# Modulation chunk 23 of layer 0 moves from TensorE to VectorE, and the first two down chunks are taken in turn by quarters

## The chip, the core and the metric

The kernel runs on one core of a Trainium2 chip. The metric is the device time of one execution in microseconds (us). The engines are named as in the profile: PE is TensorE, PEld its weight loads, DVE is VectorE, ACT is ScalarE, POOL is GpSimd, SP is SyncE, whose queue (SPq) issues the weight loads by DMA.

## The reference

A diffusion backbone of two layers over 256 latent tokens (`x`) and 256 context tokens (`ctx`), width D = 2048, inner width F = 5504. Layer 0 has a pooling mixer, layer 1 neighbourhood attention; each is followed by a gated feed-forward net with a width-3 convolution on its gate. Each layer has six modulation vectors of 2048 values per stream, from the condition vectors:

```python
ml = (silu_c @ w_mod[i] + b_mod[i]).reshape(B, 6, 1, D)
mc = (silu_cc @ w_mod[i] + b_mod[i]).reshape(6, 1, 1, D)
...
h = h + ml[:, 5] * conv_ffn(modulate(rms_norm(h, norm2_g[i]), ml[:, 3], ml[:, 4]),
                            ffn_w_gate[i], ffn_w_up[i], ffn_conv_w[i], ffn_conv_b[i], ffn_w_down[i])
if not last:
    ...
    hc = hc + mc[5] * conv_ffn(modulate(rms_norm(hc, norm2_g[i]), mc[3], mc[4]), ...)
```

The context rows go through the same weights, so both streams stand side by side as 512 columns.

## The kernel before

**Tiles.** Everything is kept transposed, features on the 128 partitions and the 512 token columns on the free axis. D is 16 input tiles (k), F is 43 tiles (f). A product of one f tile, gate (g) or up (u), takes 16 inputs; a "down" product goes the other way. Every product is three fp32r passes: high part by high, high by low, low by high, so a tile's gate has 48 matmuls. `split()` makes the two parts of a weight in SBUF: ACT casts it to the high part (L172), VectorE subtracts to get the low part (L174). It takes the buffers in turn from three pairs in `whp` and, once `extra` holds it, a fourth pair in `whx`. An input A or an activation `act` is split the same way (A: ACT L419 and DVE L420, from `nrm`, L417; `act`: ACT L513 and DVE L514).

**Weight loads.** `stage()` (L131) gives the staging buffer that has been free longest, and `load()` (DMA at L154) fills it with 512 KB. Up to the end of layer 0's partial stage, and on until `in_turn` is cleared, the loads are issued on SP's one queue in the order of the code; six `wst` buffers feed the last group.

**Modulation.** The 12,288 values of a layer are 24 chunks of 512; chunks 20 to 23 are the output gate `ml[:, 5]`, and chunk 20 + q scales the quarter q of a down chunk's output tiles (L919). In layer 0 a chunk is summed on TensorE by `mod_pe` (L228) in four steps: 1 MB is loaded (two DMAs), and eight matmuls of 32 output rows (`mod<-wm,sc`, L241) follow each step (up to chunk 20 two steps are taken together); then ACT copies the sums out (`modev`, L256), four transposes (`modt<-ident,modev`, L263) and a VectorE reduction (`modT`, L265) bring them to one column per k tile. In layer 1 the chunks are summed on VectorE by `mod_pairs` (L268): a weight tile times the condition value is added to `macc` (L299 and L301), and two STREAM_TRANSPOSE and TENSOR_REDUCE (L311, L312) and a matmul with `quad` (`quarter_sum`, L197) end it.

**Partial stage.** Gate and up of the tiles 0 to 7 are computed in four groups g while the mixer makes their inputs four at a time (`partial`, L686; matmuls L732 to 734). Tiles 0 to 5 keep their partial sums in SBUF (`part`, L747), tiles 6 and 7 in PSUM banks. At its side run `pw` (weights times shift, L714), its transposes `ptu`/`ptg` (L752) and sums `puu` (L759). A weight load of this stage is called `wcg_0`, `wcg_4`, `wcu_0` or `wcu_4` (gate or up, first or second four tiles). `between(half)` stands ahead of every half product: it pulls the modulation steps forward to a fixed rate (`need`, L785), 20 steps over the 32 halves of a group, and in the last group makes the second norm's scale (`n2v`, L390 to L392), normalises the inputs 0 to 11, and runs the gates of tiles 0 to 3 (`GATES`, halves 16, 19, 22 and 25). A gate (`gate0`, L497) needs the tile's `late` values (the norm's scale, L484 or L490, and the shift on ACT), two `g` operations on VectorE (L501, L503), a silu on ACT (L506), a product `sg` (L507) and the two parts of `act`.

**After the partial stage.** The main sequence (L923 on) makes the last four inputs and tile 6's gate, computes gate and up of tile 8 (`gu0`, L829, matmuls L844 to L846), then down chunk 0 (the tiles 0 to 3): four quarters `mg` of 48 matmuls (`down0`, L857; L907 to L909), whose weights of two loads each are split like the others. Each of the four outputs of a quarter is scaled on ACT (`dy`, L919) and added to `hl` and `hc` on GpSimd (L920). The gates of tiles 4 to 8 run between these quarters. Tiles 9, 10 and 11 follow, then down chunk 1 (the tiles 4 to 7), then the tiles 12 on. Layer 1's chunks (`pump`) start on VectorE with tile 12.

Of the kernel before, what the change touches and what calls it, by code (L numbers as in the profile page):

```python
# [17 lines left out]
P = 128  # L18
# [20 lines left out]
GATES = (16, 19, 22, 25)  # L39
# [20 lines left out]
def kernel(ctx: ExitStack, tc: tile.TileContext, xT, cxT, wmod, wg, wu, wd, wp,  # L60
# [97 lines left out]
    casts = []  # L158

    def split(ts, name, share=0, keep=False):  # L160

        parts = []
        for j, (t, n) in enumerate(ts):
            turn[0] += 1
            pools = [whp] * 3 + extra
            pool = pools[turn[0] % len(pools)]
            hi = pool.tile([P, 1024], F32R, tag="wh", name=f"{name}h{j}")
            lo = pool.tile([P, 1024], F32R, tag="wl", name=f"{name}l{j}")
            with ExitStack() as behind:
                for ins in hold:  # L170
                    behind.enter_context(tc.issue_after(ins))
                casts.append(nc.scalar.copy(hi[:, :n], t[:, :n]).ins)  # L172
                eng = nc.gpsimd if share and turn[0] % share == 0 else nc.vector
                eng.tensor_tensor(lo[:, :n], t[:, :n], hi[:, :n].bitcast(F32), op=ALU.subtract)  # L174
            parts.append((hi, lo))
        if not keep:
            used(ts)
        return parts
# [18 lines left out]
    def quarter_sum(x, n, name):  # L197


        ps = bank("d", f"{name}s")  # L200
        nc.tensor.matmul(ps[:, : 16 * n].rearrange("p (k s) -> p k s", s=n), quad, x, start=True, stop=True)
        v = ps[:, : 16 * n].rearrange("p (i b s) -> p i b s", b=4, s=n)
        return [v[32 * b : 32 * b + 32, :, b, :] for b in range(4)]
# [64 lines left out]
    def mod_pairs(todo, ring):  # L268
# [5 lines left out]
        def fetch(l, ch, m, streams, piece):  # L274
            tag = ring[len(loaded) % len(ring)]
            w = wst.tile([P, 1024], F32, tag=f"wst{tag}", name=f"wm{l}_{ch}_{piece}")
            if m == 1:
                g, j = divmod(2 * piece, 4)
                nc.sync.dma_start(w, wmod[l, ch, g, :, 512 * j : 512 * j + 1024])
# [9 lines left out]
        for i, (l, ch, m, streams, piece) in enumerate(steps):  # L289
            n = len(streams)  # L290
            while len(loaded) < min(i + 1 + ahead, len(steps)):
                fetch(*steps[len(loaded)])
            if piece == 0:
                acc = mp.tile([P, 1024], F32, tag="macc", bufs=1, name=f"macc_{l}_{ch}")
                acc = [acc, acc] if m == 2 else [acc[:, 0:512], acc[:, 512:1024]]
            for k, v in loaded[i]:
                for s in streams:
                    if k == 0:
                        nc.vector.tensor_scalar(acc[s], v, sc2[:, k, s : s + 1], None, op0=ALU.mult)  # L299
                    else:  # L300
                        nc.vector.scalar_tensor_tensor(acc[s], v, sc2[:, k, s : s + 1], acc[s],  # L301
                                                       op0=ALU.mult, op1=ALU.add)
            if ending is not None:
                ending()
                ending = None
            if piece == 8 * m - 1:
                r = mp.tile([P, 2, 16, 2], F32, tag="modr", bufs=2, name=f"modr_{l}_{ch}")
                for c in range(m):
                    for s in streams:
                        t = f0.tile([P, 512], F32, tag="t2", name=f"modu{s}_{l}_{ch}_{c}")  # L310
                        nc.vector.transpose(t, acc[s][:, 512 * c : 512 * c + 512])  # L311
                        nc.vector.tensor_reduce(out=r[:, c, :, s], in_=t.rearrange("p (k r) -> p k r", r=32),  # L312
                                                axis=AX.X, op=ALU.add)

                def ending(l=l, ch=ch, m=m, streams=streams, n=n, r=r):
                    for c in range(m):
                        finish_mod(l, ch + c, streams, quarter_sum(r[:, c, :, 0:n], n, f"modt_{l}_{ch + c}"))
            yield
        ending()
# [86 lines left out]
    A = {}  # L406

    def normalise(l, which, h_of, streams, rstd, pool, ks=range(KT), keep=A):

        for k in ks:  # L410
# [11 lines left out]
            keep[k] = a  # L422
            if l == 1 and k == 1:
                hold[:] = [ins.ins]
# [25 lines left out]
    with ExitStack() as ph0:  # L450
# [46 lines left out]
        def gate0(f, pg, pu):  # L497
# [10 lines left out]
            if f == NS - 1:  # L508
                a = mp.tile([P, 2, 512], F32R, tag="macc", bufs=1, name=f"act_{f}")
# [11 lines left out]
        with ExitStack() as phs:  # L521
# [37 lines left out]
            def mods():  # L559
# [6 lines left out]
                for q in range(4):  # L566
                    yield from mod_pe(0, 20 + q, sc, f0)
# [208 lines left out]
            for g in range(4):  # L776
# [8 lines left out]
                def between(half):  # L785
                    need(min(20 * g + LEAD + RATE * (half + 1) // 32, 20 * g + LEAD + PMAX))
# [25 lines left out]
            need(97)  # L812
# [7 lines left out]
        extra.append(whx)  # L820
# [4 lines left out]
        pump = mod_pairs([x for t in zip(two, one) for x in t], ring)  # L825

        tail = []

        def gu0(f):  # L829
            res = []  # L830
            for nm, wsrc in (("g", wg), ("u", wu)):
                parts = ld(wsrc[0, f], f"w{nm}0_{f}")
                if f > NS + 3:
                    next(pump, None)
                ps = bank("gu", f"{nm}0_{f}")
                for k in range(KT):
# [3 lines left out]
                    with ExitStack() as behind:  # L840
                        if f == NS and k == 0:
# [6 lines left out]
                    if k == 7 and f > NS + 3:  # L848
                        next(pump, None)
                res.append(ps)  # L850
# [6 lines left out]
        def down0(c, fs, acts, after=None):  # L857
            n = len(fs)
            last = c == len(chunks) - 1
            for mg in range(4):  # L860
# [34 lines left out]
                for m in range(4):  # L895
# [3 lines left out]
                    for i in range(n):  # L899
# [3 lines left out]
                        with ExitStack() as behind:  # L903
                            if c == 0 and i == 0:
# [4 lines left out]
                        nc.tensor.matmul(ps, lo[:, o : o + P], xh, start=False, stop=(i == n - 1))  # L909
# [11 lines left out]
                if after is not None:  # L921
                    after()
# [5 lines left out]
        res = gu0(NS)  # L928
        rest = [e for e in range(NS) if e not in acts]

        def more():
            e = rest.pop(0) if rest else None
            if e is not None:
                acts[e], _ = gate0(e, *late(e))

        while rest and rest[0] < 4:
            more()

        down0(0, chunks[0], [acts[f] for f in chunks[0]], more)
        while rest:  # L940
            more()
        acts[NS], sg = gate0(NS, *res)
        for c, fs in enumerate(chunks):
            if c < 2:
                continue
            if c == 3:
                in_turn.clear()
                rooms[:] = [r for r in rooms if -r not in ring]
# [677 lines left out]
```

## Time and profile before

| | |
|---|---|
| median of 3 runs | 3034.51 us (3032.35 to 3036.01) |
| profiled execution | 3033.66 us, span 3031.6 us, mean granted clock 0.996 |
| PE | 2971.9 us busy, 98% of the span |
| DVE, ACT, POOL | 64%, 45%, 26% of the span |
| DMA | 561.8 MB, 184 GB/s over the span |

The partial stage's last group runs from about 330 to 413 us of the span, tile 8 from 413 to about 439, down chunk 0 behind it. The page gives busy shares of each engine, the chain of work that ended last, and groups of instructions by line; rows of the timeline give start, duration, engine, line, output and inputs by the program's names (numbers left out where a row stands for several), and in brackets the idle time before the instruction and what ended it. A matmul's duration in a row overlaps its neighbours', so costs on PE are taken from start to start.

### The profile page before, as it was taken

The page shows a single profiled execution, that of the slowest core. Times are in us where ns is not written, and L with a number is a line of the kernel's source. Part 1 is how long each engine was busy: PE and PEld are TensorE (multiplying, and loading weights), DVE is VectorE, ACT ScalarE, POOL GpSimd, SP SyncE. Part 2 cuts the span into 40 slices and gives each one's busy share as a digit, 9 for nine tenths or more (in the row PEclk, how much of TensorE's full clock was granted, in tenths as well). Part 3 has the DMA queues.
Part 4 walks back from the last instruction along what each step waited for, and adds up shares of the span by engine and source line. Part 5 has one row for each costly group of instructions (what it writes and reads, how often), then busy time and mean ns, then how long its engine had stood idle before and what let it go on. Part 6 is the DMA issues. An engine that isn't in the chain of part 4 may idle for free.

```text
span 3031.6 us, 40905 instructions
## 1 busy us (share of the span) xinstructions
PE 2971.9 (98%) x15136; PEld 2413.7 (80%) x15136; DVE 1944.3 (64%) x2818; ACT 1377.2 (45%) x2234; POOL 797.7 (26%) x782
## 2 busy tenths in 40 slices
PE   5999999999999999999999999999999999999998
PEld 2666668888888888888888888878888888888887
DVE  4455674376584857658485657474778666666666
ACT  4433454324333242433334534343546566566665
POOL 0000003303123030311305002020003565566665
PEclk9999999999999999999999999999999999999999
DMA  9798653374665847566482433333346565555563
GB/s 395 283 363 317 231 193 98 115 245 150 204 203 165 236 148 235 159 202 209 152 257 78 127 99 123 107 120 112 112 151 204 172 199 190 193 182 188 183 193 118
DMA packets 178935, 561.81 MB, mean 185 GB/s; under 512 B 17712, under 2 KB 22576, under 8 KB 178736
## 3 DMA queue, kind: packets, MB, share of 16 engines
q1 hardware_dynamic: 178736, 559.19, 56.7%
q8 instruction: 120, 1.97, 0.3%
q14 instruction: 79, 0.65, 0.1%
HBM read 557.03 MB, written 2.10 MB: 184 GB/s over the span
## 4 chain that ended last, share of the span: by engine, by line
PE 94%; DMA 2%; POOL 1%; ACT 1%; DVE 1%; SPq 0%; issue 0%; DVEq 0%; ACTq 0%; POOLq 0%
PE g L1123 5%; PE u L1123 5%; PE d L907 5%; PE d L908 5%; PE d L909 5%; PE d L1176 4%; PE u L844 4%; PE u L845 4%; PE u L846 4%; PE g L845 4%; PE g L846 4%; PE g L844 4%; PE g L1126 3%; PE u L1126 3%; PE mod L241 2%; PE d L1180 2%
## 5 line engine op out<-in xcount | busy, mean ns | idle before, releaser
L920 POOL TENSOR_TENSOR hl<-hl,dy 128x256 f32<-128x256 f32 x160 | 148.4, 928 | 1010.4 <-ACT dy L919 1010.2
L1192 POOL TENSOR_TENSOR hl<-hl,dy 128x256 f32<-128x256 f32 x320 | 323.0, 1045 | 214.7 <-ACT dy L1190 212.4
L301 DVE SCALAR_TENSOR_TENSOR macc<-wm,sc,macc 128x512 f32<-128x512 f32 (+1 forms) x360 | 326.5, 937 | 72.2 <-DMA wm<-wmod 71.3
L919 ACT ACTIVATE dy<-d,modT 128x256 f32<-128x256 f32 x320 | 133.4, 470 | 187.5 <-PE d L909 169.2
L920 POOL TENSOR_TENSOR hc<-hc,dy 128x256 f32<-128x256 f32 x160 | 128.6, 803 | 0.0
L174 DVE TENSOR_TENSOR wd_2l<-wd,wd_2h 128x1024 fp32r<-128x1024 f32 (+1 forms) x44 | 55.6, 1270 | 108.2 <-ACT wd_2h L172 107.0
L1190 ACT ACTIVATE dy<-d,modT 128x512 f32<-128x512 f32 x160 | 104.6, 685 | 43.3 <-PE d L1180 41.8
L174 DVE TENSOR_TENSOR wd_3l<-wd,wd_3h 128x1024 fp32r<-128x1024 f32 (+1 forms) x44 | 53.4, 1234 | 77.3 <-ACT wd_3h L172 75.9
L241 PE MATMUL mod<-wm,sc 128*32 128x512 f32 x768 | 97.3, 624 | 5.6 <-DMA wm<-wmod 4.3
L1278 POOL TENSOR_TENSOR rk<-rk,rp 128x256 f32<-128x256 f32 x16 | 14.8, 927 | 317.4 <-DVE rk L1277 205.3
L174 DVE TENSOR_TENSOR wd_1l<-wd,wd_1h 128x1024 fp32r<-128x1024 f32 (+1 forms) x44 | 53.7, 1224 | 57.1 <-ACT wd_1h L172 57.1
L392 POOL TENSOR_TENSOR n2v<-n2v,minus_half 128x4 f32<-128x4 f32 x1 | 1.0, 1012 | 317.5 <-DMA wm<-wmod 317.5
L172 ACT CAST wd_1h<-wd 128x1024 fp32r<-128x1024 f32 (+1 forms) x44 | 45.3, 1031 | 77.5 <-PE u L845 53.1
L174 DVE TENSOR_TENSOR wd_0l<-wd,wd_0h 128x1024 fp32r<-128x1024 f32 (+1 forms) x44 | 53.2, 1220 | 27.5 <-ACT wd_0h L172 27.5
L1368 ACT ACTIVATE sb<-sb,nm 128x512 f32<-128x512 f32 x64 | 46.3, 723 | 51.7 <-DVE nm L1364 51.1
L907 PE MATMUL d<-act,wd_2h 128*128 128x512 f32 x172 | 67.1, 390 | 0.0
L908 PE MATMUL d<-act,wd_2h 128*128 128x512 f32 x172 | 66.9, 389 | 0.0
L909 PE MATMUL d<-act,wd_2l 128*128 128x512 f32 x172 | 66.9, 389 | 0.0
L907 PE MATMUL d<-act,wd_0h 128*128 128x512 f32 x172 | 66.9, 389 | 0.0
L908 PE MATMUL d<-act,wd_0h 128*128 128x512 f32 x172 | 66.9, 389 | 0.0
L909 PE MATMUL d<-act,wd_0l 128*128 128x512 f32 x172 | 66.9, 389 | 0.0
L907 PE MATMUL d<-act,wd_1h 128*128 128x512 f32 x172 | 66.9, 389 | 0.0
(1794 smaller groups left out, 9219.7 us busy)
## 6 DMA issues: line engine op xcount, KB each, us to landing
wm<-wmod SPq DMA_DIRECT2D x384, 512.0 KB, 6.4
wd<-wd SPq DMA_DIRECT2D x168, 512.0 KB, 4.4
wg<-wg SPq DMA_DIRECT2D x156, 512.0 KB, 4.6
wu<-wu SPq DMA_DIRECT2D x156, 512.0 KB, 4.6
wv<-wv SPq DMA_DIRECT2D x32, 512.0 KB, 4.0
wk<-wq SPq DMA_DIRECT2D x32, 512.0 KB, 4.0
wq<-wq SPq DMA_DIRECT2D x32, 512.0 KB, 3.8
wo<-wo SPq DMA_DIRECT2D x31, 512.0 KB, 4.5
```

Source lines behind the costliest of these rows:

```text
L174: eng.tensor_tensor(lo[:, :n], t[:, :n], hi[:, :n].bitcast(F32), op=ALU.subtract)
L301: nc.vector.scalar_tensor_tensor(acc[s], v, sc2[:, k, s : s + 1], acc[s], op0=ALU.mult, op1=ALU.add)
L844: nc.tensor.matmul(ps, hi[:, c : c + P], xh, start=(k == 0), stop=False)
L845: nc.tensor.matmul(ps, hi[:, c : c + P], xl, start=False, stop=False)
L846: ins = nc.tensor.matmul(ps, lo[:, c : c + P], xh, start=False, stop=(k == KT - 1))
L907: nc.tensor.matmul(ps, hi[:, o : o + P], xh, start=(i == 0), stop=False)
L908: nc.tensor.matmul(ps, hi[:, o : o + P], xl, start=False, stop=False)
L909: nc.tensor.matmul(ps, lo[:, o : o + P], xh, start=False, stop=(i == n - 1))
L920: nc.gpsimd.tensor_tensor(h_of(s)[:, k, :], h_of(s)[:, k, :], y[:, s], op=ALU.add)
L1123: nc.tensor.matmul(ps, hi[:, c : c + P], flat(B[k]), start=(k == 0), stop=False)
L1126: nc.tensor.matmul(ps[:, T:], lo[:, c : c + P], B[k][:, 0], start=False, stop=(k == KT - 1))
L1192: nc.gpsimd.tensor_tensor(hl[:, k, :], hl[:, k, :], y[:, q], op=ALU.add)
```

## The change

Chunk 23 is no longer summed by `mod_pe` (`LATER`). `mod_pairs` sums it for both streams on VectorE: eight loads of 512 KB into a ring of three `wst` buffers, 32 operations on `macc` (in `whx`'s buffer "wh"), two transposes and two reductions. Its pieces are advanced with tile 9 and with the down quarters, and each is ordered behind the last low part that was issued before it. Its quarter sum on TensorE stands behind quarter 2 of down chunk 1. The rate of the pumped steps in the last group goes from 20 to 15 over 32 halves.

The gates of tiles 0 to 3 leave `between`; they and tile 7's run behind tile 8's products, and 4, 5 and 8 behind tile 9's. Gate and up of tile 9 come ahead of the down chunks, and down chunks 0 and 1 are taken in turn: quarter 0 of chunk 0, quarter 0 of chunk 1, quarter 1 of chunk 0, and so on. `act_6` and `act_7` live in `whx`'s "wl" and in `mp`'s "macc", so `whx` joins `split()`'s turn only behind tile 11: until then there are three pairs. From tile 9 on the ring's three buffers are no rooms for weight loads. `in_turn` is cleared behind the quarters.

```diff
-GATES = (16, 19, 22, 25)
+LATER = (23,)
...
                 for q in range(4):
-                    yield from mod_pe(0, 20 + q, sc, f0)
+                    if 20 + q not in LATER:
+                        yield from mod_pe(0, 20 + q, sc, f0)
...
-                    need(min(20 * g + LEAD + RATE * (half + 1) // 32, 20 * g + LEAD + PMAX))
+                    need(20 * g + LEAD + (RATE if g < 3 else 19 - 4 * len(LATER)) * (half + 1) // 32)
...
-                    if g == 3 and half in GATES:
-                        e = GATES.index(half)
-                        acts[e], _ = gate0(e, *late(e))
...
-            need(97)
+            need(97 - 4 * len(LATER))
...
-        extra.append(whx)
...
+        endings = []
+        first_pump = mod_pairs([(0, ch, 1, both) for ch in LATER], ring, (whx, "wh"), last_low, endings)
...
             for k, v in loaded[i]:
                 for s in streams:
...
+                    with ExitStack() as behind:
+                        for x in (start, low_of) if home else ():
+                            behind.enter_context(tc.issue_after(x[-1]))
...
-        res = gu0(NS)
-        rest = [e for e in range(NS) if e not in acts]
...
-        while rest and rest[0] < 4:
-            more()
-
-        down0(0, chunks[0], [acts[f] for f in chunks[0]], more)
-        while rest:
-            more()
-        acts[NS], sg = gate0(NS, *res)
+        res = [gu0(NS)]
+        for e in (NS - 1, 0, 1, 2, 3):
+            acts[e], _ = gate0(e, *late(e))
+        rooms[:] = [r for r in rooms if -r not in ring]
+        res.append(gu0(NS + 1))
+        for e in (4, 5):
+            acts[e], _ = gate0(e, *late(e))
+        acts[NS], _ = gate0(NS, *res[0])
+        for mg in range(4):
+            for c in range(2):
+                down0(c, chunks[c], [acts[f] for f in chunks[c]], (mg,))
+                next(first_pump, None)
+                if (mg, c) == (2, 1):
+                    endings.pop(0)(tail)
+        acts[NS + 1], _ = gate0(NS + 1, *res[1])
+        in_turn.clear()
         for c, fs in enumerate(chunks):
             if c < 2:
                 continue
...
-            fs = [f for f in fs if f > NS]
+            fs = [f for f in fs if f > NS + 1]
             for f in fs:
                 acts[f], sg = gate0(f, *gu0(f))
+            if c == 2:
+                extra.append(whx)
+                continue
             down0(c - 1, chunks[c - 1], [acts[f] for f in chunks[c - 1]])
```

**SP's queue at the start of the last group, before** (chunk 20's loads `wm_20_...` and the first up weights `wcu_0`):

```order
L154 DMA wm_20_0_0_2899<-wmod 128x1024
L154 DMA wm_20_0_1024_2901<-wmod 128x1024
L154 DMA wm_20_1_0_2935<-wmod 128x1024
L154 DMA wm_20_1_1024_2937<-wmod 128x1024
L154 DMA wm_20_2_0_2965<-wmod 128x1024
L154 DMA wm_20_2_1024_2967<-wmod 128x1024
L154 DMA wcu_0_0_2992<-wu 128x2x512
L154 DMA wcu_0_1024_2994<-wu 128x2x512
```

The same place with the change:

```order
L154 DMA wm_20_0_0_2899<-wmod 128x1024
L154 DMA wm_20_0_1024_2901<-wmod 128x1024
L154 DMA wcu_0_0_2976<-wu 128x2x512
L154 DMA wcu_0_1024_2978<-wu 128x2x512
L154 DMA wm_20_1_0_2988<-wmod 128x1024
L154 DMA wm_20_1_1024_2990<-wmod 128x1024
L154 DMA wm_20_2_0_3033<-wmod 128x1024
L154 DMA wm_20_2_1024_3035<-wmod 128x1024
```

The two loads of `wcu_0` have moved ahead of four loads of chunk 20.

**SP's queue ahead of the stage's last weights `wcu_4`, before:**

```order
L154 DMA wm_22_2_0_3292<-wmod 128x1024
L154 DMA wm_22_2_1024_3294<-wmod 128x1024
L154 DMA wm_22_3_0_3320<-wmod 128x1024
L154 DMA wm_22_3_1024_3322<-wmod 128x1024
L154 DMA wm_23_0_0_3361<-wmod 128x1024
L154 DMA wm_23_0_1024_3363<-wmod 128x1024
L154 DMA wcu_4_0_3391<-wu 128x2x512
L154 DMA wcu_4_1024_3393<-wu 128x2x512
```

With the change:

```order
L154 DMA wm_21_2_0_3202<-wmod 128x1024
L154 DMA wm_21_2_1024_3204<-wmod 128x1024
L154 DMA wm_21_3_0_3231<-wmod 128x1024
L154 DMA wm_21_3_1024_3233<-wmod 128x1024
L154 DMA wm_22_0_0_3270<-wmod 128x1024
L154 DMA wm_22_0_1024_3272<-wmod 128x1024
L154 DMA wcu_4_0_3300<-wu 128x2x512
L154 DMA wcu_4_1024_3302<-wu 128x2x512
```

`wcu_4` stands a whole chunk earlier in the sequence of the chunk loads: behind the first step of chunk 22 and not of chunk 23.

**VectorE's order where tile 8's last inputs (`A_0_3_...`) are made, before** (`wd_0_0l` is a low part of down chunk 0's first weights, `g_6`, `sg` and `late` belong to tile 6's and 7's gates):

```order
L174 TENSOR_TENSOR wd_0_0l_3724<-wd_0_0_0_3719,wd_0_0h_3723 128x1024
L420 SCALAR_TENSOR_TENSOR A_0_3_3555<-nrm_3556,modT_15_2894,A_0_3_3555 128x256 x2
L420 SCALAR_TENSOR_TENSOR A_0_3_3563<-nrm_3564,modT_15_2894,A_0_3_3563 128x256
L503 SCALAR_TENSOR_TENSOR g_6_3571<-late_0_3403,vt_71,g_6_3571 128x2x255
L420 SCALAR_TENSOR_TENSOR A_0_3_3563<-nrm_3564,modT_15_2894,A_0_3_3563 128x256
L417 SCALAR_TENSOR_TENSOR nrm_3582<-hl,modT_19_2759,n2acc 128x256
L417 SCALAR_TENSOR_TENSOR nrm_3582<-hc,modT_19_2759,n2acc 128x256
L417 SCALAR_TENSOR_TENSOR nrm_3590<-hl,modT_19_2759,n2acc 128x256
L417 SCALAR_TENSOR_TENSOR nrm_3590<-hc,modT_19_2759,n2acc 128x256
L507 TENSOR_TENSOR sg_3575<-sg_3575,late_1_3551 128x512
L420 SCALAR_TENSOR_TENSOR A_0_3_3581<-nrm_3582,modT_15_2894,A_0_3_3581 128x256 x2
L420 SCALAR_TENSOR_TENSOR A_0_3_3589<-nrm_3590,modT_15_2894,A_0_3_3589 128x256 x2
```

With the change (its line numbers: `nrm` L434, low part of A L437, `late` L508, gate L521 and L525, low part of a weight L175):

```order
L521 SCALAR_TENSOR_TENSOR g_6_3464<-late_0_3312,vt_71,g_6_3464 128x2x255
L434 SCALAR_TENSOR_TENSOR nrm_3475<-hl,modT_19_2759,n2acc 128x256
L434 SCALAR_TENSOR_TENSOR nrm_3475<-hc,modT_19_2759,n2acc 128x256
L434 SCALAR_TENSOR_TENSOR nrm_3483<-hl,modT_19_2759,n2acc 128x256
L434 SCALAR_TENSOR_TENSOR nrm_3483<-hc,modT_19_2759,n2acc 128x256
L437 SCALAR_TENSOR_TENSOR A_0_3_3456<-nrm_3457,modT_15_2894,A_0_3_3456 128x256 x2
L175 TENSOR_TENSOR wu_8l_3560<-wu_8_1024_3553,wu_8h_3559 128x1024
L525 TENSOR_TENSOR sg_3468<-sg_3468,late_1_3444 128x512
L508 TENSOR_TENSOR late_0_3612<-cg_998,n2acc 128x512
L508 TENSOR_TENSOR late_1_3616<-cu_1270,n2acc 128x512
L437 SCALAR_TENSOR_TENSOR A_0_3_3474<-nrm_3475,modT_15_2894,A_0_3_3474 128x256 x2
L437 SCALAR_TENSOR_TENSOR A_0_3_3482<-nrm_3483,modT_15_2894,A_0_3_3482 128x256 x2
```

The two `late` operations of tile 7 now stand between tile 6's gate and the last inputs, and the 1024 low part there is tile 8's own.

On PE the down quarters of the change run with the first half's parts for three output tiles (18 matmuls of tiles 0 and 1 of the chunk's four) ahead of the second half's.

More of the change, by code (lines that the diff above doesn't have):

```diff
@@ L195, in by_row, with quarter_sum @@
         return ps.rearrange("p (i j c) -> p i c j", i=4, j=4)[:, :, 0:2, :]
-    def quarter_sum(x, n, name):
+    def quarter_sum(x, n, name, last=()):
         ps = bank("d", f"{name}s")
-        nc.tensor.matmul(ps[:, : 16 * n].rearrange("p (k s) -> p k s", s=n), quad, x, start=True, stop=True)
+        with ExitStack() as behind:
+            for ins in last:
+                behind.enter_context(tc.issue_after(ins))
+            nc.tensor.matmul(ps[:, : 16 * n].rearrange("p (k s) -> p k s", s=n), quad, x, start=True, stop=True)
         v = ps[:, : 16 * n].rearrange("p (i b s) -> p i b s", b=4, s=n)
@@ L278, in fetch @@
                 g, j = divmod(2 * piece, 4)
-                nc.sync.dma_start(w, wmod[l, ch, g, :, 512 * j : 512 * j + 1024])
+                with ExitStack() as behind:
+                    for ins in fetched[-1:] if home or (l, ch) == (1, 0) else ():
+                        behind.enter_context(tc.issue_after(ins))
+                    nc.sync.dma_start(w, wmod[l, ch, g, :, 512 * j : 512 * j + 1024])
                 loaded.append([(2 * piece + i, w[:, 512 * i : 512 * i + 512]) for i in range(2)])
@@ L507, in gate0 @@
             nc.vector.tensor_tensor(sg, sg, pu, op=ALU.mult)
-            if f == NS - 1:
-                a = mp.tile([P, 2, 512], F32R, tag="macc", bufs=1, name=f"act_{f}")
+            if f in (NS - 2, NS - 1):
+                pool, tag = (whx, "wl") if f < NS - 1 else (mp, "macc")
+                a = pool.tile([P, 2, 512], F32R, tag=tag, bufs=1, name=f"act_{f}")
             else:
@@ L840, in gu0 @@
                     with ExitStack() as behind:
-                        if f == NS and k == 0:
+                        if f <= NS + 1 and k == 0:
                             for x in tail:
@@ L849, in gu0 @@
                         next(pump, None)
+                    elif k == 7 and f == NS + 1:
+                        next(first_pump, None)
                 res.append(ps)
```

51 lines of the change are left out of this document (27 added, 24 removed).

## The prediction, as put on record

> **What bounds the kernel now.** I read the page first, for the busy shares and the chain that ended last.
>
> ```profile
> PE 2971.9 (98%) x15136; PEld 2413.7 (80%) x15136; DVE 1944.3 (64%) x2818; ACT 1377.2 (45%) x2234; POOL 797.7 (26%) x782
> PE 94%; DMA 2%; POOL 1%; ACT 1%; DVE 1%; SPq 0%; issue 0%; DVEq 0%; ACTq 0%; POOLq 0%
> ```
>
> TensorE (PE) is the bound nearly everywhere, so an edit is worth the TensorE work it removes plus the TensorE waits it ends. The table by stage, around the end of the partial stage, shows where waits are left (columns: stretch, its length, busy us of PE, PEld, DVE, ACT, POOL, granted clock, DMA share, GB/s).
>
> ```profile
> 340.00:350.00 10.00, 7.67 (x35) 4.45 (x34) 5.70 (x14) 1.91 (x3) 1.01 (x1) 0.83 0.17 67
> 390.00:400.00 10.00, 7.18 (x50) 3.48 (x50) 9.99 (x21) 9.94 (x20) 0.00 (x0) 1.00 0.99 351
> 420.00:430.00 10.00, 7.33 (x28) 4.75 (x27) 8.93 (x21) 8.13 (x18) 0.00 (x0) 1.00 0.21 65
> 450.00:460.00 10.00, 10.00 (x46) 8.29 (x45) 6.46 (x6) 6.10 (x14) 6.40 (x7) 1.00 0.32 105
> ```
>
> The first three stretches are not full, and all lie where the change works; in the last, inside a down quarter, PE is full. So I price four things before 430 and ask whether the new order behind it stays full.
>
> **Part 1: chunk 23 leaves TensorE.** The PE timeline around one of its four steps, and the start and end of one 48-matmul product (u of tile 8):
>
> ```profile
> 408.81 0.39 PE L732 MATMUL cu<-Ad,wcu_4h 128*128 128x512 f32 x1
> 409.12 1.06 PE L241 MATMUL mod<-wm,sc 128*32 128x512 f32 x8
> ...
> 410.46 0.62 PE L734 MATMUL cu<-Ad,wcu_4l 128*128 128x512 f32 x2
> ...
> 428.65 0.39 PE L844 MATMUL u<-A,wu_8h 128*128 128x512 f32 x1
> ...
> 439.54 0.39 PE L907 MATMUL d<-act,wd_0h 128*128 128x512 f32 x1
> ```
>
> A full matmul takes (439.54 - 428.65) / 48 = 0.227 us. From 408.81 to 410.46 lie two of them (one row left out) and the step: 1.65 - 0.45 = 1.2 us. Four steps: **4.8 us** off TensorE. Its four transposes (about 0.4 us, as 342.48 to 342.86 below) are replaced by one quarter sum:
>
> ```profile
> L201 PE MATMUL modt_0s<-modr,quad x2: 191/232/274, 635.4 to 635.4; 128*128 128x32 f32 x2
> L301 DVE SCALAR_TENSOR_TENSOR macc<-wm,sc,macc x360: 732/746/1294, 595.2 to 1581.4; 128x512 f32<-128x512 f32 x120, 128x1024 f32<-128x1024 f32 x60
> L299 DVE TENSOR_SCALAR macc<-wm,sc x24: 473/679/747, 592.7 to 1544.4; 128x512 f32<-128x512 f32 x16, 128x1024 f32<-128x1024 f32 x8
> L311 DVE STREAM_TRANSPOSE modu<-macc x32: 658/682/707, 623.7 to 1634.3; 128x512 f32<-128x512 f32 x32
> L312 DVE TENSOR_REDUCE modr<-modu x32: 634/655/678, 625.0 to 1636.2; 128x16 f32<-128x512 f32 x32
> ```
>
> Two records of 0.23 us: even. The same sum for layer 1 gives VectorE's price: 2 x 0.47 + 30 x 0.75 + 2 x 0.68 + 2 x 0.66 = 26 us, spread over tiles 8 and 9 and six down quarters (some 108 us in which TensorE is meant to be full). Nobody needs chunk 23 before the last quarter. Its eight loads (4 MB) and tile 9's four go into stretches like 450 to 460, with a DMA share of 0.32. I cost both at nothing; if that cover is gone, the slower rival below is what it costs.
>
> **Part 2: the wait at 340.** PE rows, the DMA queue's row just ahead of wcu_0's issue, and the chain from that issue on:
>
> ```profile
> 339.76 0.39 PE L734 MATMUL cg<-Ad,wcg_0l 128*128 128x512 f32 x1
> 342.48 0.63 PE L263 MATMUL modt<-ident,modev 128*128 128x128 f32 x4 [2.33 <-DVE n2v L390]
> 342.86 0.47 PE L732 MATMUL cg<-Ad,wcg_0bh 128*128 128x512 f32 x1
> 347.05 0.40 PE L734 MATMUL cg<-Ad,wcg_0bl 128*128 128x512 f32 x1
> ```
>
> ```profile
> 327.56 2.79 SPq L154 DMA_DIRECT2D wm<-wmod  x4
> ```
>
> ```profile
> 330.39 9.02 DMA wcu<-wu
> 339.44 1.05 ACT wcu_0h L172
> 340.51 1.22 DVE wcu_0l L174
> ```
>
> VectorE's queue holds the low part of wcu_0 ahead of the norm's n2v. wcu_0 was issued behind four chunk loads, so it landed at 339.44, and n2v came late. PE lost 342.48 - 339.76 - 0.23 = 2.5 us; then the clock was down (0.83 in the table) and 11 steps took 4.19 us in place of 2.5: 1.7 more. With 15 in place of 20 pumped steps, wcu_0 is issued right behind chunk 20's first two loads, at 327.56, where before two wm loads stood. Eight loads are in flight and one lands every 1.2 us (9.02 / 7.5 ahead of it, an estimate), so four places are worth 4.8 us: it lands near 334.6. Cast and low part end near 337, before the sums of cg end at 340. Both losses go: **4.2 us** (bounds 0, if the load lands no earlier, and 4.2).
>
> [...]
>
> **Part 3: the waits at 391 to 400.**
>
> ```profile
> 391.88 0.66 PE L263 MATMUL modt<-ident,modev 128*128 128x128 f32 x4 [0.34 <-ACT modev L256]
> 394.56 0.59 PE L714 MATMUL pwu<-wcu,sh 128*32 128x256 f32 x2 [0.44 <-DVE modT L265]
> 396.54 1.09 PE L714 MATMUL pwu<-wcu,sh 128*32 128x256 f32 x14 [1.39 <-DMA wcu<-wu]
> 399.86 1.07 PE L241 MATMUL mod<-wm,sc 128*32 128x512 f32 x8 [0.65 <-DMA wm<-wmod]
> ```
>
> ```profile
> 389.62 0.89 SPq L154 DMA_DIRECT2D wcu<-wu  x2
> ```
>
> Together 2.8 us. Six buffers feed this stage, and wcu_4 takes the pair that the third step ahead gives back: chunk 22's third step (about 389.5) before, chunk 21's third now. Before, 5 us of work lay between release and use, and the load needed 6.9 (389.62 to 396.54). Now 17 matmuls (3.9), two steps (2.4) and two transpose groups (0.8) lie between: 7.1 us. It just covers; I take **2.8 us** off (bounds 0 and 2.8).
>
> **Part 4: tile 8's last four inputs.**
>
> ```profile
> 422.03 0.39 PE L844 MATMUL g<-A,wg_8h 128*128 128x512 f32 x1
> 422.85 0.50 PE L845 MATMUL g<-A,wg_8h 128*128 128x512 f32 x1 [0.43 <-DVE A L420]
> ```
>
> ```profile
> 417.69 0.19 DVE L759 TENSOR_REDUCE puu<-ptu 128x8 f32<-128x32 f32 x1 [0.25 <-PE ptu L752]
> 417.80 0.68 DVE L490 TENSOR_TENSOR late<-cu,n2acc 128x512 f32<-128x512 f32 x1
> 418.39 0.48 DVE L417 SCALAR_TENSOR_TENSOR nrm<-hl,modT,n2acc 128x256 f32<-128x256 f32 x1
> 418.79 0.48 DVE L417 SCALAR_TENSOR_TENSOR nrm<-hc,modT,n2acc 128x256 f32<-128x256 f32 x1
> 420.13 0.74 DVE L501 SCALAR_TENSOR_TENSOR g<-late,vt,g 128x510 f32<-128x510 f32 x1
> 420.79 1.22 DVE L174 TENSOR_TENSOR wd_0l<-wd,wd_0h 128x1024 fp32r<-128x1024 f32 x1
> 421.93 1.27 DVE L420 SCALAR_TENSOR_TENSOR A<-nrm,modT,A 128x256 fp32r<-128x256 f32 x3
> ```
>
> From 422.03 to 428.65 stand 12 matmuls (2.7 us): **3.9 us lost** to VectorE, which starts its last stretch only at puu, behind the transposes ptu. Start to start, a late is 0.6, an nrm 0.4, a g 0.66, a 1024 low part 1.14, an A 0.39. Before, that stretch sums to 0.6 + 8 x 0.4 + 1.3 + 1.14 + 8 x 0.39 + 0.6 + 0.2 = 10.2 and ends 15.0 us behind the tile's start at 412.98. Now it holds two more late (11.3), but ptu stands behind 8 of the tile's matmuls rather than 16, so it starts 1.8 us earlier: 14.2. That is **0.9 us** better, not 3.9: the four gates that leave the stage ran ahead of this stretch, not in it. (Bounds -1, if the gate of tile 7 gets in between, and 3.9, if it starts early.)
>
> **Part 5: what comes behind.** The gates of tiles 0 to 3 and 7 now run on VectorE beside g_8 to u_9. From tile 8's last input to the low part of act_3 the order puts five gates (2.5 each by the prices above), five 1024 low parts, 14 macc pieces and little else: about 29 us. TensorE has u_8, g_9, u_9 (144 x 0.227 = 32.7 us) and 19 matmuls of the first quarter (4.3): 37. The margin of 8 us shrinks by the waits between ACT and DVE inside a gate.
>
> ```profile
> 455.76 0.69 DVE L507 TENSOR_TENSOR sg<-sg,part 128x512 f32<-128x512 f32 x1 [0.76 <-ACT sg L506]
> 457.72 1.27 DVE L514 TENSOR_TENSOR act<-sg,act 128x512 fp32r<-128x512 f32 x1 [1.27 <-ACT act L513]
> ```
>
> A gate alone waits 2 us; five would lose 10 against a margin of 8. They are interleaved, so the cost lies between 0 and 2; and the down quarters run on three pairs of high and low buffers, not four. In each quarter the order puts 18 matmuls (4.1 us) on the first half's parts before the second half is needed, so a second half that comes 4 us late costs nothing. I charge **1.0 us** for both, near the lower end because every cover is longer than its load.
>
> The last row shows also that an act takes 1.27 us beside GpSimd's adds (0.6 alone). [...] It does not enter the sum while the cover holds; the slower rival uses the row.
>
> **Sum.** 4.8 + 4.2 + 2.8 + 0.9 - 1.0 = 11.7 us. The profiled execution took 3033.66 us (span 3031.6 and 2.1 around it), 0.85 under the median of 3034.51; taken off that median, 3022.8 us.
>
> **Rivals.** (a) The waits move along: loads are issued when TensorE gives buffers back, so a faster stage also asks earlier, and parts 2 and 3 return nothing: 3034.5 - 4.8 - 0.9 + 1.0 = 3029.8. For it: DMA stands at 0.99 in 390 to 400. Against: the two loads really stand earlier in the queue. (b) The slow clock spell stays, with only the 2.5 us gone: 3024.5. (c) VectorE reaches tile 8's stretch early enough and all 3.9 go: 3019.8. (d) **Slower**: the second low part of each down quarter is late. Behind a freed buffer stand a cast (1.05), macc pieces at 1.29 and the low part at 1.27 or more on a full VectorE; with the cover of 4.1 + 2.7 us, eight quarters must each wait 1.5 us before the gain of 11.7 is gone. With three macc pairs ahead (7.7) the chain is 10.0 and each waits 3.2: 3022.8 + 8 x 3.2 = 3048. Against: VectorE is busy 6.46 of 10 in a quarter with a gate, and only one macc pair stands between two low parts.
>
> **Chances.** Forecast 0.58, (a) 0.11, (b) 0.10, (c) 0.13, (d) 0.08. The range reaches from all bounds at their best (4.8 + 4.2 + 2.8 + 3.9 = 15.7, and 1.8 for the spread of the runs, 3032.35 to 3036.01), 3017, to (a) and 1 us, 3031; only (d) lies outside. A measurement of this kernel tells about 0.2% (6 us) from no change: faster 0.81, same 0.11 (that is (a)), slower 0.08.
>
> **What would show it.** Right: no mod matmul for chunk 23; no wait for n2v and full clock behind it; wcu_4 landed before pwu; tile 8 starts near 400, still with a few us of waits for A; PE full from there through the eight quarters. Wrong: a wait for wcu_0 or wcg_4 (its loads also moved), a wait for act or wd low parts at the quarters, or macc waiting for wm at VectorE's head with low parts behind it.

## The result, and the profile after

The change took 3025.91 us (median of 7 runs, 3023.41 to 3028.70) against 3034.51 (7 runs, 3032.35 to 3037.43): a ratio of **0.9973, 95% interval 0.9963 to 0.9982**, or 8.6 us less (5.5 to 11.2 by the interval). The forecast, 11.7 us less, lies just outside that interval: the gain is clear of the noise and smaller than forecast. The profiled execution has a span of 3024.1 us.

The page of the change, its busy shares and the chain that ended last: TensorE is the bound as before, VectorE has 24 us more to do.

```profile
PE 2967.3 (98%) x15102; PEld 2413.7 (80%) x15102; DVE 1967.8 (65%) x2856; ACT 1376.4 (46%) x2233; POOL 795.5 (26%) x782
PE 94%; DMA 1%; DVE 1%; POOL 1%; ACT 1%; issue 1%; SPq 0%; DVEq 0%; ACTq 0%; POOLq 0%
```

From run to run the program reaches its last partial group anywhere from 327.6 to 333.2 us, and what follows tile 12 varies from 2439.7 to 2443.6 us. Both lie outside the change, so I compare **the stretch** from the group's first `cg` matmul to tile 12's first `g` matmul: 329.98 to 591.86 before (261.88 us), 327.56 to 581.41 after (253.85), 8.03 us less. TensorE's waits in that stretch, for the change:

```profile
PE g L865 <- DVE A L437: 2.6, 1, 2.6
PE modt L267 <- ACT modev L260: 1.4, 1, 1.4
PE cg L752 <- ACT Ad L691: 1.0, 1, 1.0
```

Of the waits of before, those for wcu_4, its neighbours and n2v are gone; one for A stays, and one for modev is new. The table by stage of the change (same columns as in the prediction):

```profile
330.00:340.00 10.00, 9.29 (x45) 5.83 (x43) 5.23 (x11) 3.26 (x7) 1.01 (x1) 0.83 0.87 313
390.00:400.00 10.00, 10.00 (x55) 6.06 (x48) 4.87 (x9) 5.61 (x11) 0.00 (x0) 1.00 0.85 300
410.00:420.00 10.00, 7.43 (x25) 5.25 (x25) 9.96 (x18) 8.46 (x16) 0.00 (x0) 0.83 0.17 55
440.00:450.00 10.00, 10.00 (x46) 8.29 (x45) 10.00 (x15) 4.18 (x6) 0.00 (x0) 1.00 0.49 154
```

390 to 400 is full now. The granted clock is down twice, near 330 and near 415, where before it was down once. At 440 to 450 TensorE is full, but VectorE is full too (10.00): the room behind tile 8 is nearly used up.

The wait near 340, on PE and on ACT:

```profile
338.90 0.39 PE L754 MATMUL cg<-Ad,wcg_0l 128*128 128x512 f32 x1
340.73 0.66 PE L267 MATMUL modt<-ident,modev 128*128 128x128 f32 x4 [1.44 <-ACT modev L260]
```

```profile
330.63 1.06 ACT L173 CAST wcu_0h<-wcu 128x1024 fp32r<-128x1024 f32 x1
...
339.15 1.04 ACT L173 CAST wcu_0h<-wcu 128x1024 fp32r<-128x1024 f32 x1 [6.74 <-issue]
340.10 0.58 ACT L260 COPY modev<-mod 128x512 f32<-128x512 f32 x1
```

Counted from the group's start, wcu_0's first half is cast 6.4 us earlier (3.07 us behind it against 9.46), more than the 4.8 of the forecast. But the order of ACT now has the second cast ahead of modev too, and that one starts at 339.15, just when the last matmul of wcg_0's first half is over. So modev is late: 340.73 - 338.90 - 0.23 = 1.6 us lost where 2.5 were lost before.

Tile 8, on PE (the wait and what follows) and on VectorE (the last operations ahead of the late A):

```profile
411.99 0.49 PE L864 MATMUL g<-A,wg_8h 128*128 128x512 f32 x1
415.05 0.50 PE L865 MATMUL g<-A,wg_8h 128*128 128x512 f32 x1 [2.57 <-DVE A L437]
...
416.93 0.63 PE L864 MATMUL u<-A,wu_8h 128*128 128x512 f32 x1
```

```profile
403.90 0.19 DVE L269 TENSOR_REDUCE modT<-modt 128x8 f32<-128x32 f32 x1 [0.17 <-PE modt L267]
...
411.19 1.22 DVE L175 TENSOR_TENSOR wu_8l<-wu,wu_8h 128x1024 fp32r<-128x1024 f32 x1
412.32 0.68 DVE L525 TENSOR_TENSOR sg<-sg,late 128x512 f32<-128x512 f32 x1
412.93 0.68 DVE L508 TENSOR_TENSOR late<-cg,n2acc 128x512 f32<-128x512 f32 x1
413.53 0.68 DVE L508 TENSOR_TENSOR late<-cu,n2acc 128x512 f32<-128x512 f32 x1
414.12 1.66 DVE L437 SCALAR_TENSOR_TENSOR A<-nrm,modT,A 128x256 fp32r<-128x256 f32 x4
```

VectorE goes without a gap from the transposes (403.9) to the last A (415.8), 12 us, as it took 11 before; TensorE gets there early and waits.

### The profile page after: what moved, and what is told of

It reads as the page before. It is cut to its first block, busy times and chain, and to the rows that moved or that the text cites. A ratio compares the mean times of both kernels' runs of the same rounds, so it can differ in the third digit from the quotient of the medians.

```text
span 3024.1 us, 40882 instructions
## 1 busy us (share of the span) xinstructions
PE 2967.3 (98%) x15102; PEld 2413.7 (80%) x15102; DVE 1967.8 (65%) x2856; ACT 1376.4 (46%) x2233; POOL 795.5 (26%) x782
## 4 chain that ended last, share of the span: by engine, by line
PE 94%; DMA 1%; DVE 1%; POOL 1%; ACT 1%; issue 1%; SPq 0%; DVEq 0%; ACTq 0%; POOLq 0%
PE g L1145 5%; PE u L1145 5%; PE d L929 5%; PE d L931 5%; PE d L930 5%; PE d L1198 4%; PE u L864 4%; PE u L865 4%; PE u L866 4%; PE g L865 4%; PE g L866 4%; PE g L864 4%; PE g L1148 3%; PE u L1148 3%; PE mod L245 2%; PE d L1202 2%
## 5 line engine op out<-in xcount | busy, mean ns | idle before, releaser
L312 DVE SCALAR_TENSOR_TENSOR macc<-wm,sc,macc 128x512 f32<-128x512 f32 (+1 forms) x390 | 352.1, 933 | 71.3 <-DMA wm<-wmod 70.3
L175 DVE TENSOR_TENSOR wd_2l<-wd,wd_2h 128x1024 fp32r<-128x1024 f32 (+1 forms) x44 | 57.3, 1308 | 101.7 <-ACT wd_2h L173 100.8
L175 DVE TENSOR_TENSOR wd_3l<-wd,wd_3h 128x1024 fp32r<-128x1024 f32 (+1 forms) x44 | 53.3, 1229 | 81.2 <-ACT wd_3h L173 80.0
L175 DVE TENSOR_TENSOR wd_1l<-wd,wd_1h 128x1024 fp32r<-128x1024 f32 (+1 forms) x44 | 54.7, 1246 | 55.3 <-ACT wd_1h L173 55.3
L175 DVE TENSOR_TENSOR wd_0l<-wd,wd_0h 128x1024 fp32r<-128x1024 f32 (+1 forms) x44 | 53.8, 1231 | 25.8 <-ACT wd_0h L173 25.8
L1390 ACT ACTIVATE sb<-sb,nm 128x512 f32<-128x512 f32 x64 | 46.2, 722 | 50.8 <-DVE nm L1386 50.1
L929 PE MATMUL d<-act,wd_1h 128*128 128x512 f32 x172 | 66.9, 389 | 0.0
L930 PE MATMUL d<-act,wd_1h 128*128 128x512 f32 x172 | 66.9, 389 | 0.0
```

Of the source, the lines that this page charges most:

```text
L175: low_of[:] = [eng.tensor_tensor(lo[:, :n], t[:, :n], hi[:, :n].bitcast(F32), op=ALU.subtract).ins]
L929: nc.tensor.matmul(ps, hi[:, o : o + P], xh, start=(i == 0), stop=False)
L930: nc.tensor.matmul(ps, hi[:, o : o + P], xl, start=False, stop=False)
```

## The experiments

My theory after this comparison: (1) chunk 23's steps are worth their 5 us; (2) the earlier loads ended the waits at wcu_4; (3) the moved gates cost and give nothing; (4) modev and the last inputs wait only for their places in the orders of ACT and VectorE; (5) a slow clock spell follows some waits, by phase. The rivals: the gain is that of the moved gates and the interleaved quarters, and VectorE, busy 9.8 us or more of every 10 from 420 to 450, takes back whatever is saved ahead of it. Stretch, number of 3.4 us slow spells in it, and time ratio to before with its interval:

| run | stretch | slow spells | ratio |
|---|---|---|---|
| before | 261.9 | 1 | 1 |
| the change | 253.9 | 2 | 0.9973 (0.9963 to 0.9982) |
| e1 chunk 23 left out | 253.7 | 2 | 0.9975 (0.9965 to 0.9986) |
| e2 chunk 23 on TensorE | 260.7 | 3 | 0.9997 (0.9988 to 1.0007) |
| e3 old rate | 255.7 | 4 | 0.9986 (0.9976 to 0.9995) |
| e4 four gates back | 263.0 | 4 | 1.0009 (0.9999 to 1.0018) |
| e5 inputs first | 258.1 | 2 | 0.9996 (0.9987 to 1.0006) |
| e6 modev first | 255.0 | 4 | 0.9976 (0.9965 to 0.9986) |
| e7 both orders | 257.1 | 3 | 0.9983 (0.9974 to 0.9993) |
| e8 e2 with inputs first | 257.4 | 2 | 0.9981 (0.9972 to 0.9991) |
| e9 both orders, sum later | 248.4 | 0 | 0.9964 (0.9950 to 0.9977) |
| e10 the change again | 253.8 | 2 | 0.9971 (0.9962 to 0.9981) |
| e11 two gates back | 258.3 | 2 | 0.9998 (0.9989 to 1.0007) |

### e1: chunk 23 left out

```diff
-        first_pump = mod_pairs([(0, ch, 1, both) for ch in LATER], ring, (whx, "wh"), last_low, endings)
+        first_pump = iter(())
+        modT[0, 23] = modT[0, 22]
...
-                    endings.pop(0)(tail)
+                    pass
```

> The stretch from the last group's first cg matmul to tile 12's first g matmul took 261.9 us in the profile of before and 253.9 in that of the change; all numbers here are of that stretch. This kernel leaves chunk 23's sum out altogether and uses chunk 22's values in its place, so VectorE's 26 us and the eight loads are gone. Theory (the cover is longer than the load): nothing comes of it but the quarter sum, 253.0 to 254.0. Rival (VectorE's sum or its loads cost TensorE time behind tile 8): 252 or less, with fewer waits behind tile 8.

253.65 us, the same waits as the change. The 0.2 us of difference are the quarter sum; VectorE's 26 us and the eight loads cost nothing where they stand.

### e2: chunk 23 back on TensorE

```diff
-LATER = (23,)
+LATER = ()
...
-                if (mg, c) == (2, 1):
+                if (mg, c) == (2, 1) and endings:
```

> Chunk 23 goes back to TensorE (pumped at a rate of 19 over 32 halves); gates, tile 9 and the quarters stay as in the change. Theory: the four steps and their transposes cost 5.2 us again, and some of the waits for wcu_0 and wcu_4 that went (0 to 3.7): 259 to 263 us for the stretch, near the 261.9 of before. Rival (the moved gates and the interleaved quarters bring the gain): 256 or less.

260.70: within the forecast, but only in part by the road it took. No wait for wcu_0 or wcu_4 came back. The run takes 6.8 us more than the change. The chunk's own steps and transposes are about 5 of it, and tile 8 is 4.2: its gate takes 19.7 us against 15.5, slow clock included (0.59 granted from 420 to 430). Against that, this run has neither the change's wait for modev nor its early slow spell. VectorE's rows of this run in tile 8:

```profile
411.12 1.23 DVE L175 TENSOR_TENSOR wu_8l<-wu,wu_8h 128x1024 fp32r<-128x1024 f32 x1 [0.51 <-ACT wu_8h L173]
415.58 0.19 DVE L269 TENSOR_REDUCE modT<-modt 128x8 f32<-128x32 f32 x1 [3.23 <-PE modt L267]
```

VectorE, whose order is fixed, stands idle for 3.2 us for the last chunk's transposes, with the last inputs queued behind them. So the last chunk step does not only take TensorE's time: it sets when VectorE starts for tile 8.

### e3: the old rate of the steps

```diff
-                    need(20 * g + LEAD + (RATE if g < 3 else 19 - 4 * len(LATER)) * (half + 1) // 32)
+                    need(20 * g + LEAD + (RATE if g < 3 else 20) * (half + 1) // 32)
```

> Chunk 23 stays on VectorE, but the last group's steps are pumped at the old rate of 20, so wcu_0's loads stand behind chunk 20's first six loads again, as before. Theory (the earlier loads end waits of their own): the wait for n2v or modev near 340 grows from 1.6 to about 2.5, and wcu_4 is waited for again; the stretch takes 254.8 to 257.6 us. Rival (the waits only move along, the loads' places do not matter): 253.9 as in the change.

255.65, but the waits named did not come. wcu_0 was late again (its cast waited for the DMA until 338.69), yet TensorE ran at half clock for 6.8 us just then and was late itself. wcu_4, issued behind all of chunk 22, was not waited for. So the advance by a whole chunk was not needed to end that wait (one step remains: this place is behind chunk 22's fourth step, that of before behind chunk 23's first). Two more slow spells, at most 1.7 us each (3.41 us at a granted clock of 0.50), are enough for the 1.8 us above the change.

### e4: the four gates back in the stage

```diff
+GATES = (16, 19, 22, 25)
...
+                    if g == 3 and half in GATES:
+                        e = GATES.index(half)
+                        acts[e], _ = gate0(e, *late(e))
...
-        for e in (NS - 1, 0, 1, 2, 3):
+        for e in (NS - 1,):
```

> The gates of tiles 0 to 3 run inside the partial stage again (halves 16, 19, 22 and 25); all else is the change. Theory (they ran ahead of the last inputs' stretch on VectorE, not in it, and their cover behind tile 8 is long enough): within 1 us of 253.9 for the stretch, the wait for A in tile 8 still about 3. Rival (their leaving makes the last inputs earlier): the wait for A grows to 4 or more and the stretch to 255 or more.

263.02: my theory's point (3) falls. The waits of the run for A, for wcu_4's parts and for tile 8's weights (modev's, 1.7 us against 1.4 in the change, left out):

```profile
PE g L869 <- DVE A L438: 2.2, 1, 2.2
PE cu L753 <- ACT wcu_4h L174: 2.0, 1, 2.0
...
PE g L868 <- ACT A L437: 1.6, 1, 1.6
PE g L868 <- ACT wg_8h L174: 1.4, 1, 1.4
PE cu L755 <- DVE wcu_4l L176: 1.3, 1, 1.3
```

wcu_4 was issued 51.3 us into the group (382.75 - 331.47) against 50.8 in the change (378.38 - 327.56), so it is not the load. VectorE at that place:

```profile
385.96 2.50 DVE L503 TENSOR_TENSOR part<-part,n2acc 128x512 f32<-128x512 f32 x4
388.37 0.75 DVE L520 SCALAR_TENSOR_TENSOR g<-part,vt,g 128x510 f32<-128x510 f32 x1
389.02 0.69 DVE L503 TENSOR_TENSOR part<-part,n2acc 128x512 f32<-128x512 f32 x1
389.63 2.36 DVE L176 TENSOR_TENSOR wcu_4l<-wcu,wcu_4h 128x1024 fp32r<-128x1024 f32 x2
```

The low parts that TensorE needs next stand behind the gates' work. The fixed order of TensorE differs here too (it takes wcu_4's matmuls earlier, ahead of the chunk's transposes and pwu), so how much is the gates' time and how much the order isn't separated.

### e11: two gates back

Only `GATES = (16, 19)`, tiles 0 and 1.

> As the run with the gates back in the stage (263.0 us for the stretch), but only those of tiles 0 and 1 (halves 16 and 19). Theory (in the stage VectorE and ScalarE are full, and each gate there delays wcu_4's parts and the last inputs by its own time): about half of the 9.2 us comes back, 256 to 260. Rival (one wait decides, that of wcu_4's parts behind the gates of tiles 2 and 3): 254.5 or less.

258.33, 4.5 us above the change and half of e4's 9.2, as forecast; the rival's 254.5 is refuted. The waits are the same kinds (wcu_4's cast 1.6 and low part 0.5, A 4.0 in three pieces). The half is in part the spells' doing: e4 has two more than this run and the change, and with at most 1.7 us taken off for each of the two, e4 loses 5.8 us and this run 4.5. In the time the ratios rise from 0.9973 to 1.0009 with four gates and 0.9998 with two. So two gates cost more than half of what four do, and a loss in proportion to the gates' time isn't shown.

### e5, e6 and e7: two waits taken away by order alone

```diff
-        r6 = late(NC)
-        normalise(0, 3, h_of, both, rstd, f0, range(12, 14))
-        acts[NC], sg = gate0(NC, *r6)
-        normalise(0, 3, h_of, both, rstd, f0, range(14, KT))
+        normalise(0, 3, h_of, both, rstd, f0, range(12, KT))
+        vector_behind[:] = last_low
+        r6 = late(NC)
+        vector_behind.clear()
+        acts[NC], sg = gate0(NC, *r6)
```

e6 has, in `partial`, for the last group's first up weights:

```diff
+                        elif g == 3 and fa == 0:
+                            parts = split(ts[:1], f"wc{nm}{g}_{fa}", keep=True)
+                            hold[:] = [EVICT[0, 15]]
+                            parts += split(ts[1:], f"wc{nm}{g}_{fa}b", keep=True)
+                            hold.clear()
```

> The change, with tile 8's last four inputs written ahead of the gates of tiles 6 and 7 in VectorE's order; no work is added or left out. Stretch as before (first cg of the last group to tile 12; 261.9 before, 253.9 with the change). Theory (those inputs stand 12 us behind the transposes only because of what VectorE does in between, and a slow clock spell follows the wait): the 3.1 us of wait and the 1.7 of the spell go, 248.5 to 251 us. Rival (ACT, or the gates that now come later, take the time back behind tile 8): 253 or more, with waits at the quarters.

> The change, with the second cast of wcu_0 ordered behind the copy of chunk 15's sums (modev) on ScalarE. Theory (the 1.6 us wait near 340 is modev queued behind a cast that waits for a buffer of the three pairs): the wait goes, 252.0 to 252.6 us for the stretch. Rival (the second half of wcu_0 is then late): a wait for wcu_0's second half, 253.9 or more. The slow spell near 330 is put by its own phase, 1.7 us either way.

> Both orders together. Theory: the two gains add, 247 to 249.5 us for the stretch, some 13 us faster than before in the time. Rival (the earlier tile 8 is taken back by what VectorE has still to do for the quarters): 250.5 or more, with waits for act or weights in the first quarters.

e5: 258.11, the rival. The wait for A is gone (tile 8's gate takes 11.8 us), but TensorE waits in the first quarter:

```profile
456.68 0.50 PE L930 MATMUL d<-act,wd_0h 128*128 128x512 f32 x1 [1.14 <-DVE act L533]
465.28 0.79 PE L929 MATMUL d<-act,wd_0h 128*128 128x512 f32 x1 [6.50 <-ACT dy L942]
```

The pieces of chunk 23 are ordered behind the last input's low part; with that part early they slipped ahead of the gates. In VectorE's order 22 of them stand ahead of act_3, against 12 in the change. act_3 came late, and ACT copied the first outputs (dy, which frees their banks) only behind the gates that were late with it.

e6: the wait for modev is gone, which shows that it was the order of the two; but the stretch took 255.0 where 252.0 to 252.6 was expected, with four slow spells where the change had two, and the time can't be told from the change's. e7 shows the size with one spell in the same place as the change: 11.58 us from the group's start to modt against 13.17, **1.6 us**. Its total, 257.14, carries e5's waits again (6.5 and 1.1).

### e8: chunk 23 on TensorE, inputs first

> Chunk 23 on TensorE as in the run with it put back (260.7 us for the stretch, 8 of them lost in tile 8), with the last inputs ahead of the gates. Theory (putting the chunk back cost little of its own; the loss was VectorE's stretch behind later transposes): 252 to 255 us, and 2 to 5.2 above the run with the same order and chunk 23 on VectorE. Rival (the chunk's steps are what costs): 258 or more.

257.44, between both, and 0.7 us below e5, the run with the same order, where 2 to 5.2 above it was expected: one wait of 2.2 us for A is left, since the inputs still stand behind the transposes. With it and two spells the run is not the clean price of the chunk that I wanted.

### e9: both orders, and the sum later

```diff
+FROM = 2
...
+        last_low[:] = [gate_low[FROM]]
         rooms[:] = [r for r in rooms if -r not in ring]
         res.append(gu0(NS + 1))
```

(`gate_low[f]` is the low part of tile f's act. The edits of e5 and e6 are in this run, too.)

> The last inputs ahead of the gates, modev ahead of the second cast, and now chunk 23's pieces on VectorE only behind tile 2's act (five of them ahead of act_3 and not some 24). Theory (in the run with the inputs ahead the pieces had slipped in front of the gates, and act_3 and the first outputs' copies came late for it): no wait for act or dy in the quarters, 246 to 250 us for the stretch, some 13 us faster than before in the time. Rival (VectorE has simply too much to do until the quarters, in whatever order): waits in the first two quarters again, 253 or more.

248.41, the only run without a slow spell in the stretch. Its waits:

```profile
PE d L936 <- ACT dy L949: 2.2, 1, 2.2
PE cg L759 <- ACT Ad L693: 1.0, 1, 1.0
```

The length is as expected, and one wait for dy is left that the theory excluded. So VectorE's work does fit, in the right order. The median of 3023.34 us is 11.2 below that of before in the same set of runs, where some 13 was expected, and stands beside 3026.31 of the change; the intervals of the two ratios overlap, so a gain over the change is shown in the stretch (5.4 us, of which the change's two spells can be 3.4) and not in the time.

### e10: the change again

> The change itself once more. Theory (its order of instructions is fixed, and slow clock spells come by the phase of a clock that runs freely): the same waits to 0.1 us, modev 1.4 and A 2.6, and a stretch that differs from 253.9 only by spells of about 1.7 us each: 252 to 257. Rival (the waits themselves vary): other waits, or a stretch outside that.

253.84 us, waits of 1.44 and 2.57, spells at the same two places: the stretch is steady. In e5 and e11, whose order is the same up to that wait, the first spell did not come, so its place does depend on the run.

## Why the forecast held, and where it missed

The forecast of 3022.8 us was 3.1 below the measured 3025.91; rival (b), 3024.5, lies nearer, though by part 2 not for its reason. Direction and most of the sum held.

**Part 1** was right: the steps are gone and the sum costs TensorE 0.2 us (from 515.64 to 516.55 its two records and three matmuls take 0.91 us, and three matmuls alone 0.68). Four steps and their transposes are 5.2 us, the quarter sum takes 0.2: 5.0 against 4.8. e1 shows that the cover holds.

**Part 2** is the step that failed in size: "Both losses go", 4.2 us. The load came early, as worked out. I did not look at what ACT would do with it: its second cast was moved ahead of modev, and 1.6 us of the 2.5 stayed (e6 and e7 took it away). Behind the wait the clock was full (1.00 from 341 to 351), as forecast. But a slow spell came at the group's start, 330.2 to 333.7, over before the wait began near 339, where the profile of before had none; by the last section that is a chance of the run. It took the 1.7 us back: rival (b)'s size, not its cause, since the spell that it said would stay did go. The part gave 0.9 in these two profiles, and up to 2.6 without that spell.

**Part 3** had the right size: all 2.8 us went. Its cover came out as worked out, too: from wcu_4's issue to its first use lie 7.2 us (378.38 to 385.61) where 7.1 were counted. But it isn't shown that the load's place is what was needed. e2 and e3 have the loads one step ahead of their place before, not a whole chunk, and don't wait there either; in e2 only 5.1 us lie between issue and use, about as before, but the second load landed 5.5 us behind the first one's issue and not 6.9. e4 and e11, with the loads early and gates back in the stage, do wait there, for the parts of wcu_4. So the leaving of the gates is the likelier cause, and I had put it at nothing. That is argued from these runs: how the gates made the loads of before late was not traced.

**Part 4** said 3.0 us of wait would be left; 2.8 was. That is partly luck, since its own prices (a start 1.8 us earlier, two `late` at 0.6 more) give a gain of 0.6 and not 0.9. What it left out is the slow spell behind the wait, from 415.57 to 418.98: 1.7 us. Its sentence that the gates "ran ahead of this stretch, not in it" is true of the rows quoted, and misled me: the gates cost elsewhere (e4).

**Part 5** charged 1.0 us and nothing was lost: 384 matmuls and the sum took 87.3 us from 450.58 to 537.89. The margin was thin all the same. e5 used it up with ten pieces in the wrong place. Rival (d) named late weights; what came late there were act_3 and dy.

The sum as measured: 5.0 + 0.9 + 2.8 + 0.8 (the wait for A, 3.9 to 3.1 with its neighbours) - 1.7 = 7.8, against 8.0 in the stretch. Rival (a), that parts 2 and 3 would return nothing (a gain of 4.7), lies outside the measured interval.

The four corners of chunk 23 (on TensorE or VectorE) and the gates (in the stage or behind it): 261.9 with neither moved (before), 260.7 with the gates alone (e2), 263.0 with the chunk alone (e4), 253.9 with both. Neither alone gave a measurable time. The corners aren't pure: tile 9 ahead, the interleaved quarters and the three pairs of buffers are in all but before. And they differ in slow spells (1, 3, 4 and 2, at most 1.7 us each); taken off, they would be some 260, 256, 256 and 250, gains of 4, 4 and 10 us by this estimate. So by it most of what makes both together worth more than the sum is that waits left in place brought spells with them.

## What to carry to other kernels

Before counting a wait as gone, ask which instruction is next in the fixed order of the engine that was late, and what that one waits for: an earlier load let a cast ahead of the copy that was needed. TensorE and VectorE were both nearly full here (47.4 and 48.9 us busy of the 50 from 400 to 450 in the change), and neither move alone gave a measurable time (ratios 0.9997 and 1.0009); the wait that stayed in tile 8 had a slow spell of 1.7 us behind it, so price the moves together. Work that is put "behind the last X" moves forward when X does; pin it to what it must not delay.

## What the runs showed of the clock

In the stretch, the granted clock of these runs went to 0.50 for 3.41 us at a time, or a multiple of it (6.8 us in e3). The steps of 3.41 us just ahead of a spell and the spells themselves, in the change and then before (PE's busy time is the number behind the length, the granted clock the one behind POOL's):

```profile
326.83:330.24 3.41, 2.41 (x13) 1.86 (x14) 3.41 (x11) 3.41 (x9) 0.00 (x0) 1.00 1.02 315
330.24:333.65 3.41, 3.41 (x9) 2.34 (x7) 3.38 (x5) 2.17 (x5) 0.00 (x0) 0.50 1.03 379
412.16:415.57 3.41, 0.84 (x3) 0.49 (x4) 3.41 (x8) 3.05 (x8) 0.00 (x0) 1.00 0.47 150
415.57:418.98 3.41, 3.41 (x9) 2.55 (x9) 3.38 (x6) 2.65 (x4) 0.00 (x0) 0.50 0.03 8
```

```profile
340.02:343.43 3.41, 1.08 (x8) 0.90 (x8) 2.65 (x5) 1.89 (x3) 0.73 (x1) 1.00 0.47 190
343.43:346.84 3.41, 3.41 (x10) 2.67 (x9) 2.35 (x8) 0.00 (x0) 0.28 (x1) 0.50 0.00 0
```

In these three places TensorE was busy 0.84 to 2.41 us of the 3.41 ahead of a spell. Within a trace the spells lie whole steps of 3.413 us apart, far beyond the stretch too: in the change those that begin at 330.24, 415.57 and 2200.74 are 25 and 523 steps apart (85.33 and 1785.17 us), before those at 343.43 and 1654.15 are 384 (1310.72 us). Against the program the steps lie differently in each run: one begins 2.68 us behind the group's first `cg` in the change (330.24 - 327.56), and 3.21 before (333.19 - 329.98).

I cut each of the 13 traces, at the edges of its spells, into steps of 3.41 us, from 8 us ahead of the last group to tile 12: 978 steps at full clock. In each I took PE's busy time without the one-column matmuls of the norm's sums (`n2s`; eight of them near 330 have 1.05 us, 0.14 of it beside other matmuls). It was 1.80 us or less in all 22 steps that a spell follows, and 1.87 or more in all 956 others. With `n2s` counted the two kinds overlap (up to 2.64 against 1.94 and more); why is open. So in the stretch of these runs a step in which TensorE was busy for about half or less (1.80 of 3.41 us, counted so) had the slow clock behind it.

By these counts, what looked like chance goes with where the steps fall. The waits of 2.33 us before and 2.57 in the change each fell into one step and had a spell behind them, so the first cost 2.5 + 1.7 = 4.2 us. e9's wait of 2.2 us for dy fell across two steps, with 2.31 and 2.35 us busy, and cost no more than itself (granted clock 1.00 from 455 to 465). The group's start leaves a step close to 1.8 us: it held 1.50 us in the change, with a spell behind it, and 2.03 before, with none.
